# Layer 1 of a two-layer diffusion block: the first products of the feed-forward part by seven block products for eight, the gate row put into the second weights, and the attention values kept in float32

## The chip, the core and the metric

The kernel runs on one core of one Trainium2 chip. The metric is the device time of one execution in microseconds (us); lower is better. Names used below: PE is TensorE (matrix products), PEld its weight loads, DVE is VectorE, ACT is ScalarE, POOL is GpSimd, SP issues the DMAs. PSUM is the memory into which PE writes its sums, SBUF the memory from which every engine reads its operands.

## What is computed

One sample of 512 latent tokens (x) and 256 context tokens goes through two layers of width 1024, each with a mixer and a SwiGLU feed-forward part. All values are float32. Layer 0 works on all 768 tokens; behind layer 1's mixer only the 512 latent tokens are left.

```python
def _diff_attend(q, k, v, lam):              # layer 1: 8 heads, two score maps each
    s = einsum('bqhad,bkhad->bhaqk', q, k) * HEAD_DIM ** -0.5
    p = softmax(s)
    a = p[:, :, 0] - lam * p[:, :, 1]
    return einsum('bhqk,bkhe->bqhe', a, v)   # v: 128 wide

def _odd_mixer(...):
    q, k, v = split(h @ w_in)                # q and k: RMS norm by head, latent tokens rotated
    o = _rms(_diff_attend(q, k, v, lam), subln_w) * (1.0 - lam_init)
    return o @ w_out

def _swiglu(h, w_in, w_out):                 # w_in 1024 x 5632, w_out 2816 x 1024
    gate, up = split(h @ w_in, 2)
    return (silu(gate) * up) @ w_out

# per layer: x = x + gate1 * mixer(norm(x)); x = x + gate2 * swiglu(norm(x))
```

## The kernel before

**Precision.** A large product is made of three: each float32 operand is split into a rounded part ("hi", type fp32r) and the rest ("lo"), and PE adds hi x hi, hi x lo and lo x hi in PSUM. ACT makes hi (a cast), DVE or POOL makes lo (source minus hi). The same form splits weights (`unit`, L303 and L304), activations (`hT[0]` and `hT[1]`) and the hidden rows (`split`, L397 and L398). Products of plain float32 operands also exist: in layer 0 the attention's probabilities times values (L548); the trace has two instructions for each of those.

**Layer 1's mixer.** `in_proj1` runs over eight heads and six tiles of 128 tokens: 24 matmuls (L384 to L386), a copy out of PSUM (`qkv`), the values split into hi and lo (`vv`, L594 and L595), then `qk_norm_rope`: squares, sums by head, the inverse root on POOL (`rs_q`), the product with it on DVE (L363), then two products for q and two for k (L372, L374) and one sum. `attend1` makes two score maps per head and token tile, joins them (`e`), transposes six blocks of 128 x 128 on PE (`ppt`), splits them into `PTh` and `PTl` and multiplies: PTh by both parts of v (256 columns, L653) and PTl by the hi part of v (128 columns, L654). Two more operations add the halves.

**Layer 1's feed-forward part.** `norm_hT` first norms four tiles of tokens and writes them, transposed and split, into `hT`. `ffn` then loops over 11 pairs of 128-wide hidden blocks. For a pair it loads 512 KB pieces of gate and up weights and of the way out (`wgr`, `wur`, `wdr`) and splits them; for each block, PE makes gate and up for all 512 tokens (`pg`, `pu`: 8 k-steps x 3 matmuls of 512 columns, L738); ACT takes silu, DVE multiplies and splits into `hdh`, `hdl`. The way out is 8 half rows per pair (4 token tiles x 2 halves), 6 matmuls each into `dps` (L771 to L773); `residual` multiplies each by the gate row `g` (L391) and adds it to x (L392). In the first block gate and up are made for 256 tokens at a time, so that they can start before the last tiles are normed. The last two pairs share their way out. POOL does nothing in this loop.

**What sets the order.** A scheduler that plays the program through in its own model of time fixes the order on each engine when the kernel is built. Each engine then runs its list strictly in order, with semaphore waits. The number of buffers of each name (`bufs`) bounds how far one engine may run ahead of another.

Of the kernel before, what the change touches and what calls it, by code (L numbers as in the profile page):

```python
# [10 lines left out]
F32 = mybir.dt.float32  # L11
F32R = mybir.dt.float32r
# [6 lines left out]
P = 128  # L19
# [16 lines left out]
PBUF0 = 6  # L36
PBUF = 4
# [27 lines left out]
def backbone(es: ExitStack, tc: tile.TileContext, x, c, ctx, c_ctx, mod_w, mod_b, norm_mix_w, norm_ffn_w,  # L65
# [39 lines left out]
    def f32(ap):  # L105
        return ap.bitcast(F32)
# [38 lines left out]
    def rsqrt(ss, n, inv, tag):  # L145

        r = small.tile([P, n], F32, name="rs_" + tag, tag="rs_" + tag)
        nc.gpsimd.tensor_scalar(r, ss, inv, EPS, ALU.mult, ALU.add)
        nc.gpsimd.tensor_tensor(r, r, neghalf[:, :n], ALU.pow)
        return r  # L150
# [114 lines left out]

    def norm_steps(t, xt, l, f, pool, tags=(("nh", 2), ("nhc", 2)), room=None):
# [62 lines left out]

    def rotate(raw, nq, nk, t, w, tb, pool):  # L330
# [23 lines left out]
    def qk_norm_rope(ps, nq, nk, t, w, tb, pool):  # L354

        n = nq + nk
        sq = pool.tile([P, n * HD], F32, name="sq", tag="qz", bufs=2)
        nc.scalar.activation(sq, ps[:, :n * HD], AF.Square)
        ss = small.tile([P, n], F32, name="qss", tag="qss")
        nc.vector.tensor_reduce(ss, sq.rearrange("p (h d) -> p h d", d=HD), AX.X, ALU.add)  # L360
        r = rsqrt(ss, n, 1.0 / HD, "q")
        y = pool.tile([P, n, HD], F32, name="qy", tag="qy", bufs=2)
        nc.vector.tensor_tensor(y, ps[:, :n * HD].rearrange("p (h d) -> p h d", d=HD), bc(r, 2, HD), ALU.mult)  # L363
        parts = [p for p in ((0, 0, nq), (1, nq, nk)) if p[2]]
        if t >= NTX:
            for j, h0, m in parts:
                nc.vector.tensor_tensor(y[:, h0:h0 + m], y[:, h0:h0 + m], bc(w[:, j, :], 1, m), ALU.mult)
            return y
        z = pool.tile([P, n, HD], F32, name="qz", tag="qz", bufs=2)
        for j, h0, m in parts:  # L370
            sn = tb[:, j, t, 1, :].rearrange("p (a b) -> p a b", b=2)
            nc.vector.tensor_tensor(z[:, h0:h0 + m].rearrange("p h (a b) -> p h a b", b=2),  # L372
                                    swap_pairs(y[:, h0:h0 + m]), bc(sn, 1, m), ALU.mult)
            nc.vector.tensor_tensor(y[:, h0:h0 + m], y[:, h0:h0 + m], bc(tb[:, j, t, 0, :], 1, m), ALU.mult)  # L374
        nc.vector.tensor_add(y, y, z)
        return y

# [22 lines left out]

    def transposed_probs(Pt, heads, tiles, pool):

        res = []
        per = 4 // heads
        for g0 in range(0, len(tiles), per):
            grp = tiles[g0:g0 + per]
            m = len(grp)
            pt = tr_tile("ppt", [P, per, heads, P])
            for a, kc in enumerate(grp):
                for hh in range(heads):  # L410
                    nc.tensor.transpose(pt[:, a, hh, :], Pt[hh][:, kc * P:(kc + 1) * P], ident)
            hi, lo = split(pool, pt[:, :m], [P, m, heads, P], "PT", 2)
            for a in range(m):
                res.append((hi[:, a], lo[:, a]))
        return res
# [155 lines left out]
    def in_proj1(h, tabs, wp, st, wh, qp):  # L571
        w, tb = tabs
# [9 lines left out]
        vv = st.tile([P, NT, 2, P], F32R, name="vv", tag="vv")  # L582
# [3 lines left out]
        for t in CTX_FIRST:  # L586
            nq = 2 if t < NTX else 0
            n = 384 if nq else 256
# [4 lines left out]
            v = raw[:, n - P:n]  # L593
# [31 lines left out]
    def attend1(h, t, state, o_t, nlam, subln, mp):  # L625
# [22 lines left out]
        PT = transposed_probs(E[:1], 1, list(range(NT)), mp)  # L648
        av = acc_tile("av", 256, one=1)
        vt = [4, 5, 0, 1, 2, 3]  # L650
        for a, (hi, lo) in enumerate(PT):
            v = vv[:, vt[a]].rearrange("p a d -> p (a d)")
            nc.tensor.matmul(av, hi[:, 0], v, start=a == 0, stop=False)  # L653
            nc.tensor.matmul(av[:, 0:P], lo[:, 0], v[:, 0:P], start=False, stop=a == len(PT) - 1)  # L654
        o1 = mp.tile([P, P], F32, name="o1", tag="o1", bufs=2)
        nc.scalar.activation(o1, av[:, P:2 * P], AF.Copy, scale=rc[:, 0:1])
        oc = o_t[t][:, h * P:(h + 1) * P]
        nc.vector.scalar_tensor_tensor(oc, av[:, 0:P], rc[:, 0:1], o1, ALU.mult, ALU.add)
        ss = small.tile([P, 1], F32, name="oss", tag="oss")
# [50 lines left out]
    def ffn(l, xs, ntok, wp, fp, done, mods=()):  # L710
# [6 lines left out]
        for p in range(NF // 2):  # L717
# [59 lines left out]
            wo, hid = [], []  # L777

# [156 lines left out]
    tabs = rope_tables(wp.pool, od_qn[0], od_kn[0])  # L935
# [53 lines left out]
    room = ctx_room([P, 2, KT, P], F32, "nroom")  # L989
    for t in range(NTX):  # L990
        norm_hT(t, xs[t], 1, 1, None, room=[z[:, t % 2] for z in room])
# [65 lines left out]
```

## Time and profile before

| | us |
|---|---|
| time, median of 3 runs (1862.53 to 1865.8) | 1865.1 |
| time of the profiled execution | 1865.25 |
| its span, first to last instruction | 1863.5 |
| PE busy in the span | 1760.2 |
| DVE busy | 1162.2 |
| POOL busy | 789.8 |
| ACT busy | 716.5 |

1.75 us of the profiled execution lie outside its span. Busy times of one engine overlap with those of the others. The durations of single matmuls overlap too (the next starts while the last drains), so that the pace of PE is read from starts, or from a run of n matmuls in the chain of waits, and not from the mean duration. The stages in the trace, by their place in the span: layer 0's mixer up to about 450 us, its feed-forward part to 1012, layer 1's mixer and way out to 1476, the norm and the loop of layer 1's feed-forward part from there to the end.

### The profile page before, as it was taken

The page shows a single profiled execution, that of the slowest core. Times are in us where ns is not written, and L with a number is a line of the kernel's source. Part 1 is how long each engine was busy: PE and PEld are TensorE (multiplying, and loading weights), DVE is VectorE, ACT ScalarE, POOL GpSimd, SP SyncE. Part 2 cuts the span into 40 slices and gives each one's busy share as a digit, 9 for nine tenths or more (in the row PEclk, how much of TensorE's full clock was granted, in tenths as well). Part 3 has the DMA queues.
Part 4 walks back from the last instruction along what each step waited for, and adds up shares of the span by engine and source line. Part 5 has one row for each costly group of instructions (what it writes and reads, how often), then busy time and mean ns, then how long its engine had stood idle before and what let it go on. Part 6 is the DMA issues. An engine that isn't in the chain of part 4 may idle for free.

```text
span 1863.5 us, 25986 instructions
## 1 busy us (share of the span) xinstructions
PE 1760.2 (94%) x9910; PEld 1459.6 (78%) x9910; DVE 1162.2 (62%) x1927; ACT 716.5 (38%) x1470; POOL 789.8 (42%) x852
## 2 busy tenths in 40 slices
PE   6999999998999999899999889999998899999998
PEld 4877776666778888788888788999886688888887
DVE  4665455445268876667771767888876556566563
ACT  6556555434211112112211555676665332222220
POOL 2864545521099986735561655655543200000000
PEclk9999999999999999999999889999999899999999
DMA  9112222302533234424330211111103133223231
GB/s 314 42 41 77 83 93 91 100 23 81 180 114 101 93 100 146 138 91 136 103 124 14 96 38 57 35 38 48 49 19 107 46 113 108 85 91 113 69 113 46
DMA packets 152477, 165.64 MB, mean 89 GB/s; under 512 B 16480, under 2 KB 139936, under 8 KB 152352
## 3 DMA queue, kind: packets, MB, share of 16 engines
q1 hardware_dynamic: 152000, 163.77, 27.6%
q8 instruction: 78, 1.28, 0.3%
q14 instruction: 47, 0.39, 0.1%
q10 hardware_dynamic: 352, 0.21, 0.0%
HBM read 159.73 MB, written 4.22 MB: 88 GB/s over the span
## 4 chain that ended last, share of the span: by engine, by line
PE 74%; DVE 9%; ACT 5%; POOL 4%; DMA 3%; issue 3%; SPq 0%; POOLq 0%; ACTq 0%; DVEq 0%
PE pg L738 14%; PE pu L738 14%; PE dps L771 5%; PE dps L773 5%; PE dps L772 5%; PE inps L384 4%; PE inps L385 3%; PE inps L386 3%; PE av L548 3%; PE ppt L538 2%; PE sc L504 2%; PE ops L705 2%; PE ops L707 2%; PE ops L706 2%; PE av L653 1%
## 5 line engine op out<-in xcount | busy, mean ns | idle before, releaser
L738 PE MATMUL pg<-hT,wgh 128*128 128x512 f32 (+1 forms) x720 | 246.6, 391 | 3.1 <-ACT hT L288 3.1
L738 PE MATMUL pu<-hT,wuh 128*128 128x512 f32 (+1 forms) x720 | 243.2, 388 | 0.0
L391 DVE TENSOR_TENSOR rtmp<-dps,g 128x512 f32<-128x512 f32 x200 | 135.8, 687 | 163.7 <-PE dps L773 162.0
L392 DVE TENSOR_TENSOR x<-x,rtmp 128x512 f32<-128x512 f32 x188 | 198.8, 1065 | 3.8
L771 PE MATMUL dps<-wdh,hdh 128*128 128x512 f32 x440 | 177.1, 403 | 2.2 <-DVE rtmp L391 2.2
L772 PE MATMUL dps<-wdl,hdh 128*128 128x512 f32 x440 | 174.8, 397 | 0.0
L773 PE MATMUL dps<-wdh,hdl 128*128 128x512 f32 x440 | 171.9, 398 | 1.6 <-DVE hdl L398 1.6
L738 PEld LDWEIGHTS pg<-hT,wgh 128*128 128x128 f32 x720 | 135.4, 190 | 34.4 <-ACT hT L288 3.3
L738 PEld LDWEIGHTS pu<-hT,wuh 128*128 128x128 f32 x720 | 134.2, 188 | 29.6
L738 PE MATMUL pg<-hT,wgl 128*128 128x512 f32 (+1 forms) x360 | 141.4, 393 | 0.0
L738 PE MATMUL pu<-hT,wul 128*128 128x512 f32 (+1 forms) x360 | 139.7, 388 | 0.0
L384 PE MATMUL inps<-wih,hT 128*128 128x384 f32 x384 | 132.9, 346 | 0.4 <-ACT qkv L446 0.2
L397 ACT CAST hdh<-sg 128x768 fp32r<-128x768 f32 (+1 forms) x44 | 32.0, 728 | 256.5 <-DVE sg L753 256.5
L386 PE MATMUL inps<-wih,hT 128*128 128x384 f32 x384 | 130.3, 339 | 0.0
L385 PE MATMUL inps<-wil,hT 128*128 128x384 f32 x384 | 130.2, 339 | 0.0
L197 POOL TENSOR_TENSOR modw<-modw,cols 128x1024 f32<-128x1024 f32 x48 | 100.8, 2103 | 54.0 <-DMA modw<-in_mod_w_dram 53.7
L738 PE MATMUL pg<-hTc,wgh 128*128 128x256 f32 x352 | 99.5, 287 | 3.1 <-ACT hTc L288 2.4
L528 POOL TENSOR_SCALAR Pt<-Pt,rc 128x256 f32<-128x256 f32 (+3 forms) x96 | 69.2, 733 | 77.0 <-DVE rc L525 64.9
L771 PEld LDWEIGHTS dps<-wdh,hdh 128*128 128x128 f32 x440 | 83.2, 189 | 23.0 <-DVE rtmp L391 3.4
L773 PEld LDWEIGHTS dps<-wdh,hdl 128*128 128x128 f32 x440 | 83.0, 189 | 22.2 <-DVE hdl L398 2.3
L738 PE MATMUL pu<-hTc,wuh 128*128 128x256 f32 x352 | 98.1, 283 | 0.0
L772 PEld LDWEIGHTS dps<-wdl,hdh 128*128 128x128 f32 x440 | 83.3, 189 | 17.5
(230 smaller groups left out, 4486.3 us busy)
## 6 DMA issues: line engine op xcount, KB each, us to landing
modw<-in_mod_w_dram SPq DMA_DIRECT2D x96, 512.0 KB, 4.3
wgr<-in_ffn_w_in_dram SPq DMA_DIRECT2D x44, 512.0 KB, 3.4
wur<-in_ffn_w_in_dram SPq DMA_DIRECT2D x44, 512.0 KB, 3.5
wdr<-in_ffn_w_out_dram SPq DMA_DIRECT2D x44, 512.0 KB, 3.6
wir<-in_od_w_in_dram SPq DMA_DIRECT2D x96, 128.0 KB, 2.2
x<-in_x_dram SPq DMA_DIRECT2D x8, 512.0 KB, 3.5
wir<-in_ev_w_in_dram SPq DMA_DIRECT2D x16, 256.0 KB, 2.7
wor<-in_ev_w_out_dram SPq DMA_DIRECT2D x8, 512.0 KB, 4.3
```

What stands on the lines that cost most here:

```text
L197: nc.gpsimd.tensor_tensor(pr, w, bc(sk, 2, width), ALU.mult)
L384: nc.tensor.matmul(ps, hs[0][:, k, :], a, start=k == 0, stop=False)
L385: nc.tensor.matmul(ps, hs[0][:, k, :], b, start=False, stop=False)
L386: nc.tensor.matmul(ps, hs[1][:, k, :], a, start=False, stop=k == KT - 1)
L391: nc.vector.tensor_mul(tmp, ps, g[:, n * 512:(n + 1) * 512])
L392: eng.tensor_add(xt[:, n * 512:(n + 1) * 512], xt[:, n * 512:(n + 1) * 512], tmp)
L528: nc.gpsimd.tensor_scalar(p[:, :n], p[:, :n], rc[:, hh:hh + 1], 1.0, ALU.mult, ALU.mult)
L548: nc.tensor.matmul(av[64 * j:64 * j + 64, :], vv[:, vt[kc], :], PT[:, 2 * j:2 * j + 2].rearrange("p h q -> p (h q)"), start=kc == 0, stop= ...
L738: nc.tensor.matmul(ps[:, s0:s1], a, cols_T(b, s0, s1)[:, k, :], start=k == 0 and q == 0, stop=k == KT - 1 and q == 2)
L771: nc.tensor.matmul(ps, hh, a, start=j == 0, stop=False)
L772: nc.tensor.matmul(ps, hh, b, start=False, stop=False)
L773: nc.tensor.matmul(ps, hl, a, start=False, stop=j == nj - 1)
```

## The change

Layer 0 is left as it is. In layer 1:

**1. Seven products.** Gate (and, apart from it, up) of a pair is a product of a weight block of 1024 x 256 with the normed tokens, 1024 x 512. Both are cut in two along each side, and the four blocks of the result are made of seven products instead of eight (Strassen's scheme in Winograd's form). `seven_h` makes the seven token-side operands B once: four sums of blocks, and hi and lo of each. `seven_weights` makes the seven weight-side operands for each pair: four sums on POOL (`ss`, 128 x 512 elements each), and hi on ACT and lo on DVE of all seven (`sh`, `sl`, in a ring of 8). `seven_products` runs 12 matmuls of 256 columns for each product (L848), and DVE and ACT put the four blocks of the result together from PSUM (`u`, `c`). The scores' two PSUM tiles (`bank`) hold the seven products; gate and up use the same ones in turn.

**2. The gate row.** POOL multiplies the way out's weights by the gate row (L936) ahead of their split; `way_out` then needs one sum per half row (L922) where `residual` had a product and a sum.

**3. The norm.** `norm_raw` leaves the normed tokens in float32 (`hr`); their split moved into `seven_h`.

**4. Values in float32.** `vv` is one float32 copy (POOL), the transposed probabilities `PT` are copied once (ACT for four blocks, DVE for two) and multiplied in plain float32, 128 columns each (L679). One ACT operation scales the result.

**5. The norm and rotation of q and k.** `head_tables` stores the tables for q and k side by side, so that `rotate_all` needs two products and one sum for all four halves; POOL multiplies by the inverse root behind them.

```diff
+RING7 = 8
...
-        vv = st.tile([P, NT, 2, P], F32R, name="vv", tag="vv")
+        vv = st.tile([P, NT, P], F32, name="vv", tag="vv")
...
-            nc.scalar.copy(vv[:, t, 0, :], v)
-            nc.gpsimd.tensor_sub(vv[:, t, 1, :], v, f32(vv[:, t, 0, :]))
-            y = qk_norm_rope(raw, nq, 2, t, w, tb, wp)
+            nc.gpsimd.tensor_copy(vv[:, t, :], raw[:, n - P:n])
+            y, r = rotate_all(raw[:, :n - P], h0, m, t, wc, tb, wp)
+            nc.gpsimd.tensor_tensor(y, y, bc(r, 2, HD), ALU.mult)
...
-        PT = transposed_probs(E[:1], 1, list(range(NT)), mp)
-            nc.tensor.matmul(av, hi[:, 0], v, start=a == 0, stop=False)
-            nc.tensor.matmul(av[:, 0:P], lo[:, 0], v[:, 0:P], start=False, stop=a == len(PT) - 1)
...
+            if g0:
+                nc.vector.tensor_copy(PT[:, :m], pt[:, :m])
+            else:
+                nc.scalar.copy(PT, pt)
+            for a in range(m):
+                kc = g0 + a
+                nc.tensor.matmul(av, PT[:, a, :], vv[:, vt[kc], :], start=kc == 0, stop=kc == NT - 1)
...
+    ORDER7 = ("P1", "P2", "P5", "P6", "P7", "P3", "P4")
+    def seven_weights(raw, ring, room):
...
+            hi = ring.tile([P, 4, P], F32R, name="sh", tag="sh", bufs=RING7)
+            lo = ring.tile([P, 4, P], F32R, name="sl", tag="sl", bufs=RING7)
+            nc.scalar.copy(hi, src)
+            nc.vector.tensor_sub(lo, src, f32(hi))
...
+        s1 = made(a21, a22, ALU.add)          # made: nc.gpsimd.tensor_tensor
+        s2 = made(s1, a11, ALU.subtract)
+        s3 = made(a11, a21, ALU.subtract)
+        s4 = made(a12, s2, ALU.subtract)
...
+    def seven_products(ws, B, bank, n, room):
+        for name, (whi, wlo) in zip(ORDER7, ws):
+            for k in range(4):
+                for a, b, q in ((whi, bhi, 0), (whi, blo, 1), (wlo, bhi, 2)):
+                    nc.tensor.matmul(ps, a[:, k, :], b[:, k, :], start=k == 0 and q == 0, stop=k == 3 and q == 2)
+            if name == "P1":
+                nc.scalar.copy(u[:, 0, :], ps)
+            elif name == "P2":
+                nc.vector.tensor_add(c[:, 0, :], ps, u[:, 0, :])
+            elif name == "P6":
+                nc.vector.tensor_add(u[:, 1, :], ps, u[:, 0, :])
+            elif name == "P7":
+                nc.vector.tensor_add(u[:, 2:4, :], bank[0][:, 1, :, :n], bc(u[:, 1, :], 1, 2))
+                nc.vector.tensor_add(c[:, 3, :], ps, u[:, 2, :])
+        nc.vector.tensor_add(c[:, 1:3, :], bank[1][:, 0, :, :n], u[:, 2:4, :])
...
+    def seven_h(HR, room):
+        B["P1"] = parts(b11, place(0, 0, 0), place(1, 0, 0))
+        B["P2"] = parts(b21, place(0, 1, 0), place(1, 1, 0))
+        nc.vector.tensor_sub(b11, b12, b11)
+        B["P5"] = parts(b11, place(0, 0, 1), place(1, 0, 1))
+        nc.gpsimd.tensor_sub(b12, b22, b12)
+        B["P3"] = parts(b22, place(0, 1, 1), place(1, 1, 1))
+        nc.vector.tensor_sub(b22, b22, b11)
+        B["P6"] = parts(b22, *two(keep, "t2", tag="xo", bufs=6))
+        nc.vector.tensor_sub(b21, b21, b22)
+        B["P7"] = parts(b12, *two(room, "t3", tag="tt", bufs=4))
+        B["P4"] = parts(b21, *two(room, "t4", tag="tt", bufs=4))
...
+                nc.gpsimd.tensor_mul(raw, raw, g)          # way out's weights times gate row
...
+                    nc.vector.tensor_add(xh, xh, ps)       # way_out: one sum per half row
```

On DVE, in the loop of layer 1's feed-forward part, a stretch of a pair before: half rows of the way out (`rtmp`, `x_...`), the hidden rows (`hdl`) and pieces of the gate weights (`wgl`).

```order
L398 TENSOR_TENSOR hdl<-sg,hdh 128x512 [waits Activation_49]
L304 TENSOR_TENSOR wgl<-wgr,wgh 128x1024 [waits DMAHW0_49,PE_49,Activation_49]
L391 TENSOR_TENSOR rtmp<-dps,g_15389 128x512 [waits PE_49]
L392 TENSOR_TENSOR x_14893<-x_14893,rtmp 128x512 [waits DVE_49]
L391 TENSOR_TENSOR rtmp<-dps,g_15389 128x512 [waits PE_49]
L392 TENSOR_TENSOR x_14893<-x_14893,rtmp 128x512 [waits DVE_49]
L304 TENSOR_TENSOR wgl<-wgr,wgh 128x1024 [waits DMAHW1_49,PE_49,Activation_49]
```

The same engine at the same place with the change (`sl` is the lo part of a weight operand, `u` and `c` the sums out of PSUM, `x_...` the residual rows):

```order
L816 TENSOR_TENSOR sl<-ss,sh 128x512 [waits Activation_49]
L922 TENSOR_TENSOR x_14201<-x_14201,dps 128x512 [waits PE_49] x2
L816 TENSOR_TENSOR sl<-ss,sh 128x512 [waits PE_49,Activation_49] x2
L922 TENSOR_TENSOR x_14323<-x_14323,dps 128x512 [waits PE_49] x2
L856 TENSOR_TENSOR u<-bank,u 128x512 [waits DVE_49,PE_49]
L816 TENSOR_TENSOR sl<-wu,sh 128x512 [waits Activation_49]
L857 TENSOR_TENSOR c<-bank,u 128x256 [waits DVE_49]
L922 TENSOR_TENSOR x_14445<-x_14445,dps 128x512 [waits PE_49]
L858 TENSOR_TENSOR c<-bank,u 128x512 [waits PE_49]
```

The two-step residual became one step, and the lo parts and the sums out of PSUM now stand between the half rows, each behind a wait for ACT or PE.

On POOL, which in layer 1's loop had no rows before, one pair now reads (`ss` the sums of weight blocks, `wdr` the way out's weights times the gate row):

```order
L821 TENSOR_TENSOR ss<-wu 128x512 [waits DMAHW1_49,DVE_49,Pool_49]
L936 TENSOR_TENSOR wdr<-wdr,g_14734 128x1024 [waits DMAHW2_49]
L821 TENSOR_TENSOR ss<-ss,wu 128x512 [waits DVE_49,Pool_49]
L821 TENSOR_TENSOR ss<-wu 128x512 [waits DVE_49]
L936 TENSOR_TENSOR wdr<-wdr,g_14734 128x1024 [waits DMAHW3_49]
L821 TENSOR_TENSOR ss<-wu,ss 128x512 [waits DVE_49,Pool_49]
```

So POOL stands between the DMA and the splits on ACT and DVE for eight weight sums and two products a pair (the four sums of `wg` are like those of `wu`).

On PE in layer 1's mixer, before, the products of one head and token tile with the values:

```order
L654 MATMUL av<-vv,PTl 128x128 [waits DVE_49]
L653 MATMUL av<-vv,PTh 128x256
L654 MATMUL av<-vv,PTl 128x128
L653 MATMUL av<-vv,PTh 128x256
L654 MATMUL av<-vv,PTl 128x128
L653 MATMUL av<-vv,PTh 128x256
L654 MATMUL av<-vv,PTl 128x128
```

And with the change:

```order
L679 MATMUL av<-vv,PT 128x128 [waits Activation_49]
L679 MATMUL av<-vv,PT 128x128 x3
L671 MATMUL ppt<-cst,e 128x128 [waits PE_49]
L671 MATMUL ppt<-cst,e 128x128 x3
L679 MATMUL av<-vv,PT 128x128 [waits DVE_49]
L679 MATMUL av<-vv,PT 128x128
```

The first four blocks now wait for ACT's copy alone, the last two for DVE's; no lo part is waited for. Each row of L679 is a float32 product, which the trace will show as two instructions.

More of the change, by code (lines that the diff above doesn't have):

```diff
@@ L352, in rotate @@
         return y, r
[L354 to L376, printed above, removed]
     def project(ps, t, ws, c0, c1):
@@ L399, in split @@
         return hi, lo
[L401 to L415, printed above, removed]
     def weights0(b, wp, sub, new_tile=raw_tile):
@@ L586, in in_proj1 @@
         for t in CTX_FIRST:
[L587 to L588 removed]
+            h0 = 0 if t < NTX else 2
+            m = 4 - h0
+            n = 64 * m + P
             ps = acc_tile("inps", n, one=0) if h else p_sc.tile([P, 1024], F32, name="inps", tag="sc")[:, :n]
@@ new lines, in seven_h, with parts, place, two @@
+    def seven_h(HR, room):
+        def parts(src, hi, lo):
+            nc.scalar.copy(hi, src)
+            nc.vector.tensor_sub(lo, src, f32(hi))
+            return hi, lo
+        def place(j, ks, c):
+            return hT[j][0][:, 4 * ks:4 * ks + 4, 256 * c:256 * c + 256]
+        def two(pool, name, **kw):
+            return [pool.tile([P, 4, 256], F32R, name=name, **kw) for _ in range(2)]
+        b11, b21 = HR[0][:, 0:4], HR[0][:, 4:8]
+        b12, b22 = HR[1][:, 0:4], HR[1][:, 4:8]
+        B = {}
+        B["P1"] = parts(b11, place(0, 0, 0), place(1, 0, 0))
[9 more added lines that the diff above has]
+        B["P4"] = parts(b21, *two(room, "t4", tag="tt", bufs=4))
+        return B
@@ L988, in backbone @@
         oproj.sums(t)
-    room = ctx_room([P, 2, KT, P], F32, "nroom")
-    for t in range(NTX):
-        norm_hT(t, xs[t], 1, 1, None, room=[z[:, t % 2] for z in room])
     opa.close()
```

165 lines of the change are left out of this document (152 added, 13 removed).

## The prediction

> **What bounds the kernel now.** I read the busy times by stage first, since the change touches only the last two stages.
>
> ```profile
> 505.00:1012.00 507.00, 496.46 (x2659) 419.04 (x2658) 340.68 (x345) 89.35 (x104) 334.58 (x224) 0.99 0.34 109
> 1012.00:1085.00 73.00, 66.81 (x344) 57.59 (x343) 45.21 (x102) 34.26 (x58) 39.77 (x45) 0.93 0.20 64
> 1085.00:1400.00 315.00, 293.05 (x1964) 277.74 (x1962) 254.31 (x536) 205.62 (x562) 172.41 (x255) 0.96 0.14 42
> 1476.00:1512.00 36.00, 27.85 (x163) 24.82 (x163) 23.43 (x37) 18.20 (x20) 2.27 (x2) 0.86 0.46 147
> 1512.00:1843.00 331.00, 330.45 (x1418) 265.56 (x1417) 189.91 (x244) 80.53 (x96) 0.00 (x0) 1.00 0.27 86
> ```
>
> After the stretch and its length stand PE, PEld, DVE, ACT and POOL busy, PE's granted clock and the DMA share. From 1512 us on, in the loop of layer 1's feed-forward part, PE is busy for 330.45 of 331 us at full clock, DVE for 189.91, POOL not at all. That loop is bound by PE, and what it costs is the number of matmuls times their pace. The mixer (1012 to 1400) is less clear: PE sits idle for 6.2 + 21.95 = 28.1 us there, and DVE is at 81% in the longer stretch.
>
> The pace comes from the chain of waits, whose rows give the start and length of runs of matmuls:
>
> ```profile
> 1491.43 2.71 PE pu L738 x23
> 1494.49 2.71 PE pg L738 x23
> 1499.91 5.60 PE pg L738 x24
> 1505.51 5.59 PE pu L738 x24
> 1561.48 2.56 PE pg L738 x11
> 1628.64 2.56 PE pg L738 x11
> ```
>
> The first two rows are the first block, made for 256 tokens at a time: 2.71/23 = 0.118 us a matmul. The next two are of 512 columns: 5.60/24 = 0.233 us. The last two are the same place two pairs apart: 67.16 us, 33.58 us a pair. A pair before has 96 matmuls for gate and up and 48 for the way out, all of 512 columns: 144 x 0.233 = 33.6 us, which is the measured period.
>
> **The loop: PE.** A pair now has 14 products of 12 matmuls, 168 of 256 columns: 168 x 0.118 = 19.8 us for 96 x 0.233 = 22.4 us. The way out's 11.2 us stay. If PE remains the bound, a pair takes 31.0 us, 2.6 less; 11 pairs give 28 us. The price rests on the two 256-column rows, where every matmul loads a fresh weight tile, as in the seven products. The page "TensorE: Matmul & The Clock Gate" of the Trainium skill (section LDWEIGHTS) gives columns/1.2, an estimate of 107 ns for 128 columns, under the pace; those rows agree with it.
>
> **The loop: DVE and POOL.** These are the engines that take over what PE sheds.
>
> ```profile
> L391 DVE TENSOR_TENSOR rtmp<-dps,g 128x512 f32<-128x512 f32 x74 | 50.2, 690 | 74.5 <-PE dps L773 74.5
> L392 DVE TENSOR_TENSOR x<-x,rtmp 128x512 f32<-128x512 f32 x74 | 50.1, 688 | 1.3
> L304 DVE TENSOR_TENSOR wdl<-wdr,wdh 128x1024 fp32r<-128x1024 f32 x19 | 23.3, 1225 | 17.5 <-ACT wdh L303 17.5
> L304 DVE TENSOR_TENSOR wgl<-wgr,wgh 128x1024 fp32r<-128x1024 f32 x18 | 22.0, 1223 | 20.6 <-ACT wgh L303 20.6
> L398 DVE TENSOR_TENSOR hdl<-sg,hdh 128x512 fp32r<-128x512 f32 x21 | 14.5, 690 | 8.6 <-ACT hdh L397 8.2
> L375 DVE TENSOR_TENSOR qy<-qy,qz x32: 407/418/426, 1077.5 to 1387.3; 128x256 f32<-128x256 f32 x32
> L198 POOL TENSOR_TENSOR modp<-modp x16: 1263/1293/2280, 515.2 to 686.1; 128x512 f32<-128x512 f32 x16
> L197 POOL TENSOR_TENSOR modw<-modw,cols x48: 1889/1894/2873, 516.4 to 960.8; 128x1024 f32<-128x1024 f32 x48
> ```
>
> The first five are DVE's groups between 1512 and 1843 us, with POOL idle (count, busy us, mean ns); the others are single lines with minimum, median and maximum. A pair now gives DVE 30 operations of 512 elements (14 lo parts, 8 half rows, 4 sums out of PSUM, 2 products with up, 2 hidden lo parts), 2 of 1024 and 6 sums of 256. That is 30 x 0.69 + 2 x 1.225 + 6 x 0.418 = 25.7 us. Before it was 20 x 0.69 + 6 x 1.22 = 21.1 us. POOL gets 8 sums and 2 products: 8 x 1.263 + 2 x 1.889 = 13.9 us. Both fit under 31.0 us alone. But in layer 0's loop, where POOL is busy, the same DVE operations are longer (520 to 1000 us):
>
> ```profile
> L392 DVE TENSOR_TENSOR x<-x,rtmp 128x512 f32<-128x512 f32 x108 | 144.5, 1344 | 2.3
> L391 DVE TENSOR_TENSOR rtmp<-dps,g 128x512 f32<-128x512 f32 x108 | 73.3, 684 | 65.5 <-PE dps L773 63.8 <-DMA g<-gmem 1.7
> L304 DVE TENSOR_TENSOR wdl<-wdr,wdh 128x1024 fp32r<-128x1024 f32 x18 | 29.6, 1644 | 19.8 <-ACT wdh L303 19.8
> L304 DVE TENSOR_TENSOR wgl<-wgr,wgh 128x1024 fp32r<-128x1024 f32 x18 | 26.8, 1489 | 3.2 <-ACT wgh L303 3.2
> 520.00:1000.00 480.00, 469.46 (x2490) 396.66 (x2489) 339.40 (x342) 86.98 (x100) 327.88 (x220) 0.99 0.35 111
> ```
>
> The operation with both inputs in SBUF (x plus rtmp) takes 1344 for 688 ns, the one that reads PSUM 684, as before. With 18 `wul` counted like `wgl`, the excess is 108 x 0.656 + 18 x 0.419 + 36 x 0.266 = 88 us over 162 operations, 0.54 us each, at a POOL share of 327.88/480 = 68%. In the new loop 20 operations of a pair have both inputs in SBUF (18 of 512, 2 of 1024: 14.9 us), and POOL is at 13.9/32 = 43%: 20 x 0.54 x 43/68 = 6.8 us. DVE then needs 32.5 us, less what consecutive operations overlap, about 1 us (before, 21.1 us a pair by this count are 189.91 x 33.58/331 = 19.3 busy, part of it the few half rows missing in the stretch): 31.5 us, level with PE's 31.0. Two engines so close, each in order and waiting for the other, don't mesh perfectly; I take **32.0 us** a pair, an estimate: 11 x (33.58 - 32.0) = **-17.4 us**. Bounds: 31.0 (-28 us) below; above, all 20 paying the 0.656 of the row: 25.7 + 13.1 - 1 = 37.8 us a pair (+46 us).
>
> The page "SBUF — State Buffer" (section "SBUF: two separate sides") speaks against the change: DVE with two SBUF inputs and POOL hold one port pair by an exclusive lock for a whole instruction. The excess on `x<-x,rtmp` alone and not on `rtmp<-dps,g` agrees. What that would make of the time is the second rival.
>
> ACT's 80.53 us are 8.2 us a pair; 14 casts of 512 for 4 of 1024 and two copies less than double that. The DMA carries the same bytes at 27% busy. Both cost nothing. If ACT or a load were late, the ring of 8 operands covers about 8 x 12 x 0.118 = 11 us.
>
> **The start of the loop.**
>
> ```profile
> 1475.27 0.70 DVE L391 TENSOR_TENSOR ops<-ops,g 128x512 f32<-128x512 f32 x1
> 1486.62 1.22 DVE L289 TENSOR_TENSOR hT<-nroom,hT 128x1024 fp32r<-128x1024 f32 x1 [2.83 <-ACT hT L288]
> 1487.32 0.56 PE L738 MATMUL pg<-hT,wgh 128*128 128x256 f32 x1
> 1490.17 1.36 DVE L285 TENSOR_SCALAR nroom<-npt,aff,modc 128x128 f32<-128x128 f32 x4
> ```
>
> The last half row in front of the norm reaches DVE at 1475.27; PE starts on the loop at 1487.3 and covers the end of the last tile's norm (1491.5) with the first 256 tokens. The seven products allow less of that: five of the token operands need all four tiles. Behind the last norm DVE has three sums and five lo parts of 1024 (8 x 1.22 = 9.8 us), of which PE can cover two products (24 x 0.118 = 2.8 us). If the last tile is normed at 1487 (DVE no longer splits in between) to 1491.5, the last operand is there at 1497 to 1502, and the first seven products (9.9 us) end 1.4 us later: as if PE had started at 1488 to 1494. I take **+6 us**, with the DVE work for the first weights queued behind it; bounds -1 and +15.
>
> **The mixer.**
>
> ```profile
> 1240.43 0.22 PE L654 MATMUL av<-vv,PTl 128*128 128x128 f32 x1
> 1240.48 0.34 PE L653 MATMUL av<-vv,PTh 128*128 128x256 f32 x1
> 1240.66 0.23 PE L654 MATMUL av<-vv,PTl 128*128 128x128 f32 x1
> 1241.83 0.62 PE L411 MATMUL ppt<-cst,e 128*128 128x128 f32 x4
> 1242.21 0.36 PE L634 MATMUL sc<-kT,qt 128*128 128x256 f32 x1
> 280.45 1.08 PE L548 MATMUL av<-PT,vv 128*64 128x256 f32 x8
> 281.46 0.66 PE L538 MATMUL ppt<-cst,Pt 128*128 128x128 f32 x4
> L372 DVE TENSOR_TENSOR qz<-qy,rt 128x128 f32<-128x128 f32 x60 | 25.5, 465 | 0.6
> L374 DVE TENSOR_TENSOR qy<-qy,rt 128x128 f32<-128x128 f32 x60 | 18.8, 339 | 0.0
> L363 DVE TENSOR_TENSOR qy<-qkv,rs_q 128x256 f32<-128x256 f32 x30 | 21.5, 716 | 5.5 <-POOL rs_q L149 5.5
> PE av L654 <- DVE PTl L398: 7.6, 11, 2.9
> ```
>
> By starts, a block's two products take 0.23 us, 1.4 us for six. The new ones are float32: 12 instructions. Their price stands between a float32 transpose (0.38/4 = 0.095) and layer 0's float32 products (1.01/8 = 0.126): 1.1 to 1.5 us. For 32 head tiles -10 to +4 us; the first product behind a change of operand type seems to lose some 0.1 us (an estimate), so -8 to +10, and I take +3. In return DVE loses about half of L372 and L374 (two operations become one of 256; 22 us) and L363 (21.5 us), and the lo part becomes a copy of two blocks in six: over 45 of its 254 us in 1085 to 1400. PE's wait for `PTl` (7.6 us) goes. I let PE regain a third of the 28.1 us idle: -9. Net **-6 us**, bounds -25 and +12. POOL's new products with the inverse root (44 there, at most half of the 512 row's 1.26 us each: 28 us) fit beside its 172 of 315 us.
>
> **The end.** One DVE step of 0.69 us less behind the last matmul: **-0.7 us**.
>
> **The sum.** Against the profiled execution's own 1865.25 us (0.15 above the median of 1865.1): -17.4 + 6 - 6 - 0.7 = -18.1, **1847 us**.
>
> **Rivals.** *PE stays the bound outright*: a pair at 31.0, 11 us less than forecast, **1836**. For it: POOL's share would be lower than the 68% from which the excess was scaled. Against: 31.5 us of DVE work. *The port makes DVE the bound*: POOL and DVE work on the same weights at the same time, so the excess per operation doesn't shrink with POOL's share but stays at layer 0's 0.54 us. DVE then needs 25.7 - 1 + 20 x 0.54 = 35.5 us a pair, +1.9 x 11 = +21 instead of -17.4: **1886**, slower. It decides from 33.6 us a pair, where loop and forecast's other terms cancel: an excess of 0.45 us. For it: both rows of `x<-x,rtmp`; against: in layer 0 POOL hardly ever pauses. *The mixer loses*: products at the upper price and new waits for POOL's product with the inverse root, +12 for -6: **1865**. For it: PE's idle time there has many small causes, none over 7.6 us in the waits. *The change doesn't do what it says*: 256-column matmuls paced by a weight load's 190 ns (row below) would be 168 x 0.19 = 31.9 us for 19.8, +133 us or **1980**; the rows at 0.118 us, with a load each, all but exclude it.
>
> ```profile
> L738 PEld LDWEIGHTS pg<-hT,wgh 128*128 128x128 f32 x720 | 135.4, 190 | 34.4 <-ACT hT L288 3.3 <-issue 1.2
> ```
>
> **How the numbers follow.** Forecast 0.42 (its own range 1839 to 1857), PE the bound 0.18, the port 0.25, the mixer 0.14, the weight load 0.01. The range of 1831 to 1884 takes in the forecast, the mixer, most of the first rival and the nearer half of the port's; some 0.18 is left out. A difference under 0.2% (3.7 us) can't be told from none here. Faster: the forecast, the first rival and a little of the mixer, 0.61; same: half of the mixer, 0.08; slower: 0.31.
>
> **What would show it.** In the profile after: the period of a pair (33.58 us before) near 32; PE's idle time in the loop put down to `sl` (DVE) or to DVE's reads of `bank`; `sl` over 0.9 us in the mean for the port, near 0.69 without it. The forecast is wrong if 256-column matmuls leave 0.118 us, if DVE's busy share in the loop stays under 85% (then PE is the bound), or if the mixer moves by more than 15 us.

## The result and the profile after

| | before | after |
|---|---|---|
| median, on the same chip | 1863.8 us (4 runs) | 1921.1 us (4 runs) |
| profiled execution, and its span | 1865.25, 1863.5 | 1917.72, 1915.8 |

The ratio is 1.031, 95% interval 1.028 to 1.034: the change makes the kernel 57 us slower, outside the range of 1831 to 1884. In the profiled spans it is 52.3 us. Where they lie is read first by stage. These are the windows of the kernel after, with the columns of the prediction's first fence (PE, PEld, DVE, ACT, POOL busy, PE's clock, DMA share):

```profile
1085.00:1400.00 315.00, 293.06 (x2009) 277.70 (x2008) 223.43 (x390) 198.19 (x510) 196.06 (x307) 0.98 0.16 47
1463.00:1520.00 57.00, 32.80 (x202) 29.20 (x201) 52.08 (x73) 29.57 (x41) 29.82 (x21) 0.79 0.27 93
1641.95:1829.30 187.35, 164.74 (x1081) 153.44 (x1081) 151.49 (x191) 67.89 (x110) 85.04 (x51) 0.93 0.26 85
```

The last row is the steady part of the loop. PE, which was busy for 330.45 of 331 us there, is now at 88%, DVE at 81%, POOL at 45%, and PE's clock is 0.93. No engine is full. The period is read from ACT's silu, which comes once a pair; these two rows of its timeline are six pairs apart:

```profile
1624.55 1.15 ACT L942 ACTIVATE c<-c 128x512 f32<-128x512 f32 x2 [2.05 <-DVE c L858]
1849.62 1.15 ACT L942 ACTIVATE c<-c 128x512 f32<-128x512 f32 x2 [2.04 <-DVE c L858]
```

225.07/6 = 37.5 us a pair, 3.9 more than the 33.58 before: 11 x 3.9 = +43 us. The mixer ends earlier: the last matmul ahead of the norm, by its tile `ops` in the kernel before and after (minimum, median, maximum, then first and last start):

```profile
L707 PE MATMUL ops<-woh,hT x128: 388/396/793, 339.7 to 1474.8; 128*128 128x512 f32 x128
```

```profile
L731 PE MATMUL ops<-woh,hT x128: 389/396/774, 341.0 to 1462.6; 128*128 128x512 f32 x128
```

That is -12.2 us. The rest, 52.3 - 43 + 12.2 = +21.5 us, belongs to the start and end of the last stage.

**Where PE waits.** PE's waits from 1480 us on:

```profile
PE bank L848 <- DVE c L857: 45.1, 12, 6.7
PE bank L848 <- DVE hT L865: 4.4, 1, 4.4
PE bank L848 <- ACT hT L864: 3.5, 1, 3.5
PE bank L848 <- ACT u L850: 3.3, 1, 3.3
PE dps L918 <- ACT hdh L430: 3.2, 1, 3.2
```

One wait makes up 45 us: a product's first matmul waits for `c` (L857), DVE's read of P7, twelve times. It is no wait for an operand (`sl`). The timeline of one pair shows it on PE, then on DVE, then on POOL (start, length, idle time before and its releaser):

```profile
1749.44 0.28 PE L848 MATMUL bank<-t,sl 128*128 128x256 f32 x1
1754.24 0.80 PE L848 MATMUL bank<-hT,sh 128*128 128x256 f32 x2 [4.53 <-DVE c L857]
1754.84 0.41 PE L848 MATMUL bank<-hT,sl 128*128 128x256 f32 x1
1755.05 0.63 PE L848 MATMUL bank<-hT,sh 128*128 128x256 f32 x2
...
1743.23 1.83 DVE L939 TENSOR_TENSOR wdl<-wdr,wdh 128x1024 fp32r<-128x1024 f32 x1
1744.98 0.41 DVE L852 TENSOR_TENSOR c<-bank,u 128x256 f32<-128x256 f32 x1
1745.31 1.21 DVE L939 TENSOR_TENSOR wdl<-wdr,wdh 128x1024 fp32r<-128x1024 f32 x1
1746.44 2.98 DVE L816 TENSOR_TENSOR sl<-ss,sh 128x512 fp32r<-128x512 f32 x3
1749.35 2.83 DVE L816 TENSOR_TENSOR sl<-wg,sh 128x512 fp32r<-128x512 f32 x1
1752.11 0.68 DVE L856 TENSOR_TENSOR u<-bank,u 128x512 f32<-128x512 f32 x1
1752.71 1.15 DVE L816 TENSOR_TENSOR sl<-wu,sh 128x512 fp32r<-128x512 f32 x1
1753.78 0.41 DVE L857 TENSOR_TENSOR c<-bank,u 128x256 f32<-128x256 f32 x1
...
1747.26 1.62 POOL L821 TENSOR_TENSOR ss<-wu 128x512 f32<-128x512 f32 x1 [3.28 <-issue]
1748.84 2.79 POOL L936 TENSOR_TENSOR wdr<-wdr,g 128x1024 f32<-128x1024 f32 x1
1751.59 1.71 POOL L821 TENSOR_TENSOR ss<-ss,wu 128x512 f32<-128x512 f32 x1
```

The reads of PSUM (L856, L857) stand in DVE's list behind two `wdl` and four `sl`. Most of them meet an operation of POOL: the `sl` at 1749.35 takes 2.83 us for 0.69 and ends at 1752.18, 0.55 us behind POOL's product with the gate row (1748.84 + 2.79 = 1751.63). DVE makes no pause from 1743.23 to the end of L857 at 1754.19, so that it isn't late by waiting for POOL's results there. At the pace of e4's trace (0.60 us from start to start for 512 elements, 2.27 for two `wdl`) the same operations would take 6.6 us for these 11.0, an estimate. PE finished P7 at 1749.7 and stands until 1754.24. Behind the wait, three matmuls take 0.64 us where they took 0.36 (0.118 each), for 3 to 4 us. A pair is so 31.0 us of PE's work, 4.5 of waiting and 2 of slow clock.

Why does PE wait for a read of P7 at all? In the built order the products of the up set stand on PE as P1, P6, P2, P3, P4, P5, P7, and right behind P7 comes the next gate set's P1. P1 writes other columns than P7, but both lie in the same tile, `bank[0]`, and the wait is for the tile's last reader. The up set's P1 waits for such a read as well, but half rows of the way out stand in front of it and keep PE busy; so PE stands once a pair and not twice.

**How large the contention is.** DVE's groups over five pairs (1642 to 1829 us; count, busy us, mean ns):

```profile
L816 DVE TENSOR_TENSOR sl<-ss,sh 128x512 fp32r<-128x512 f32 x40 | 32.8, 838 | 9.3 <-ACT sh L815 8.7
L816 DVE TENSOR_TENSOR sl<-wg,sh 128x512 fp32r<-128x512 f32 x15 | 21.0, 1402 | 5.1 <-ACT sh L815 5.1
L947 DVE TENSOR_TENSOR c<-c 128x512 f32<-128x512 f32 x10 | 17.5, 1792 | 0.2
L939 DVE TENSOR_TENSOR wdl<-wdr,wdh 128x1024 fp32r<-128x1024 f32 x10 | 15.2, 1518 | 0.0
L816 DVE TENSOR_TENSOR sl<-wu,sh 128x512 fp32r<-128x512 f32 x15 | 12.5, 835 | 0.0
L856 DVE TENSOR_TENSOR u<-bank,u 128x512 f32<-128x512 f32 x10 | 6.8, 684 | 2.5 <-PE bank L848 2.5
```

Against 0.69 and 1.225 us, the first five lose 40 x 0.15 + 15 x 0.71 + 10 x 1.10 + 10 x 0.29 + 15 x 0.145 = 32.7 us, 6.5 us a pair; the read of PSUM (684 ns) loses nothing. The forecast had 6.8.

### The profile page after: what moved, and what is told of

It reads as the page before. It is cut to its first block, busy times and chain, and to the rows that moved or that the text cites. A ratio compares the mean times of both kernels' runs of the same rounds, so it can differ in the third digit from the quotient of the medians.

```text
span 1915.8 us, 27843 instructions
## 1 busy us (share of the span) xinstructions
PE 1756.1 (92%) x10654; PEld 1498.4 (78%) x10654; DVE 1248.7 (65%) x1909; ACT 754.5 (39%) x1525; POOL 1002.1 (52%) x1011
## 5 line engine op out<-in xcount | busy, mean ns | idle before, releaser
L848 PE MATMUL bank<-hT,sh 128*128 128x256 f32 x704 | 144.4, 302 | 58.9 <-DVE c L857 45.1
L848 PEld LDWEIGHTS bank<-hT,sh 128*128 128x128 f32 x704 | 121.0, 206 | 67.7 <-DVE c L857 48.0
L762 PE MATMUL pg<-hT,wgh 128*128 128x512 f32 x352 | 131.3, 394 | 0.0
L762 PE MATMUL pu<-hT,wuh 128*128 128x512 f32 x352 | 130.2, 391 | 0.0
L848 PE MATMUL bank<-t,sh 128*128 128x256 f32 x528 | 108.0, 300 | 1.3 <-DVE t L865 1.3
L848 PE MATMUL bank<-hT,sl 128*128 128x256 f32 x352 | 105.5, 300 | 0.0
L796 PE MATMUL dps<-wdl,hdh 128*128 128x512 f32 x264 | 104.9, 397 | 0.0
L848 PEld LDWEIGHTS bank<-t,sh 128*128 128x128 f32 x528 | 91.6, 210 | 2.9 <-DVE t L865 1.6
L816 DVE TENSOR_TENSOR sl<-ss,sh 128x512 fp32r<-128x512 f32 x88 | 79.6, 922 | 17.4 <-ACT sh L815 16.2
L322 POOL TENSOR_TENSOR wil<-wir,wih 128x768 fp32r<-128x768 f32 x42 | 79.3, 1894 | 14.2 <-ACT wih L321 13.0
## 6 DMA issues: line engine op xcount, KB each, us to landing
wir<-in_od_w_in_dram SPq DMA_DIRECT2D x96, 128.0 KB, 2.2
```

The lines of the kernel that those rows point to most:

```text
L762: nc.tensor.matmul(ps[:, s0:s1], a, cols_T(b, s0, s1)[:, k, :], start=k == 0 and q == 0, stop=k == KT - 1 and q == 2)
L796: nc.tensor.matmul(ps, hh, b, start=False, stop=False)
L816: nc.vector.tensor_sub(lo, src, f32(hi))
L848: nc.tensor.matmul(ps, a[:, k, :], b[:, k, :], start=k == 0 and q == 0, stop=k == 3 and q == 2)
```

## The experiments

Theories: **the port** (POOL's operations hold up DVE's) and **the shared tile and the list** (PE waits for reads that stand late in DVE's list, whatever makes the list late). All times are medians; "before" was 1862.7 to 1864.5 us beside them. In the table, "pair" is the time from the fourth silu of the loop to the tenth, over 6 (in e1, from PE's runs of `pg`); PE and DVE are busy us in 1620 to 1780 (160 us).

| run | time, us | ratio to before, 95% | pair | PE | DVE |
|---|---|---|---|---|---|
| after | 1921.1 | 1.028 to 1.034 | 37.5 | 141.9 | 128.0 |
| e1 mixer alone | 1855.2 | 0.993 to 0.996 | 33.6 | | |
| e2 no POOL work | 1866.7 | 1.001 to 1.002 | 33.0 | 153.1 | 116.3 |
| e3 no gate product | 1907.7 | 1.022 to 1.026 | 37.0 | 142.8 | 120.7 |
| e4 all on DVE | 1921.1 | 1.028 to 1.033 | 37.7 | 142.6 | 130.6 |
| e12 tiles split | 1890.3 | 1.013 to 1.017 | 34.8 | 148.0 | 141.6 |
| e5 more PSUM room | 1882.9 | 1.009 to 1.013 | 35.0 | 149.6 | 139.9 |
| e6 room, no POOL work | 1839.8 | 0.985 to 0.989 | 31.6 | 160.0 | 121.1 |
| e7 room, x divided | 1862.0 | 0.998 to 1.001 | 31.4 | 158.5 | 137.5 |
| e8 room, all on DVE | 1852.3 | 0.992 to 0.995 | 31.1 | 160.0 | 151.8 |
| e9 room, gate on POOL | 1856.8 | 0.994 to 0.997 | 31.7 | 158.1 | 156.5 |
| e10 as e8, norm on ACT | 1851.2 | 0.991 to 0.994 | 31.0 | 160.0 | 152.6 |
| e11 as e10, x divided | 1861.2 | 0.997 to 0.999 | 30.8 | 160.0 | 143.2 |

The silu's place within a pair floats; in e6, with PE busy throughout, the six intervals lie between 29.7 and 32.5 us, so that PE's column is the surer one there.

**e1: the mixer alone.** The changed kernel, with the norm and feed-forward part of before.

```diff
-    HR = ctx_room([P, KT, 256], F32, "hr")
...
-    ffn7(1, xs, HR, bank, wp.pool, fp.pool,
+    room = ctx_room([P, 2, KT, P], F32, "nroom")
+    for t in range(NTX):
+        norm_hT(t, xs[t], 1, 1, None, room=[z[:, t % 2] for z in room])
...
+    ffn(1, xs, NTX, wp.pool, fp.pool,
```

> The kernel before with parts 4 and 5 of the change alone (the mixer); norm and feed-forward part as before. In the trace after, the last matmul of the way out in front of the norm starts 12.2 us earlier than before (1462.6 for 1474.8 us). Theory 'the mixer gained what it shows and all of the loss is in the feed-forward part': 1863.8 - 12 = 1852 us, 1848 to 1856. Rival 'the earlier end is only shifted work, given back behind it': 1861 to 1866 us.

1855.2 us, inside the first theory's range and 9.3 us less than before beside it (6.7 to 13.2 by the interval). The mixer's gain is kept; the feed-forward change costs 1921.1 - 1855.2 = 66 us.

**e2 and e3: POOL's work left out.** Both keep the order of the operations on PE, ACT and DVE in the last nine of the eleven pairs; in the first two the scheduler built another one.

```diff
-                nc.gpsimd.tensor_mul(raw, raw, g)          # e2 and e3
...
-            s = room.tile([P, 4, P], F32, name="ss", tag="ss", bufs=3)
-            nc.gpsimd.tensor_tensor(s, a, b, op)
-            return s
+            return a                                        # e2 alone
```

> The changed kernel without POOL's work in the loop: the four sums of weight blocks are left out (each is replaced by its first block, so the products are of other numbers) and the product of the way out's weights with the gate row is left out. DVE, ACT and PE have the same operations in the same order in the loop as the changed kernel. Theory 'the port' (DVE's operations on two SBUF inputs lose time to POOL's, and the reads of PSUM queue behind them): the wait of 4.5 us before each gate or up product set goes, with the slow matmuls behind it; a pair falls from 37.4 to 31.0 to 31.8 us, sl to 0.69 us, the time to 1848 to 1865 us. Rival 'the list' (the sums out of PSUM stand behind five lo parts in DVE's list and are late whatever POOL does): the wait stays over 2 us, a pair at 34 us or more, 1885 us or more.

> The changed kernel without POOL's product of the way out's weights with the gate row (left out, so the gate doesn't act); the four sums stay on POOL. The same order on DVE. Theory 'the port', with the two 2.8 us products in the burst ahead of the late PSUM reads as its main part: the wait of 4.5 us falls to under 2 us, a pair to 33 to 35 us, 1870 to 1892 us. Variant 'the sums matter as much': a pair at 35 to 36.5 us, 1892 to 1910 us. Rival 'the list': 1912 to 1921 us.

e2 takes 54 us off, yet a pair stays at 33.0 us, between what the two theories gave. Its timeline on PE, and its waits from 1480 us on (`c` is L855 there):

```profile
1683.60 0.28 PE L846 MATMUL bank<-t,sl 128*128 128x256 f32 x1
1685.59 0.51 PE L846 MATMUL bank<-hT,sh 128*128 128x256 f32 x2 [1.72 <-DVE c L855]
1685.93 0.28 PE L846 MATMUL bank<-hT,sl 128*128 128x256 f32 x1
1686.05 0.40 PE L846 MATMUL bank<-hT,sh 128*128 128x256 f32 x2
```

```profile
PE bank L846 <- DVE c L855: 20.4, 11, 4.4
```

With POOL idle and DVE at 73%, PE still stands 1.7 us at the same place: P7 ends, DVE makes `u`, one `sl` and then `c`. Behind this shorter wait the matmuls keep their pace. So POOL's work is worth 4.5 of the 6.5 us that a pair takes over 31.0, and 2.0 are there without it. e3's time lies where the variant "the sums matter as much" had it, its pair (37.0) a little above: the gate product is 13 us of the 54, although it is a third of POOL's busy time. In the steady pairs it is 0.5 us of the 4.5, so that there nearly all of POOL's price comes from the sums. PE still waits at the same place, nine times of the eleven for 3.44 to 3.46 us (total, times and longest):

```profile
PE bank L848 <- DVE c L857: 34.1, 11, 3.5
```

**e4: POOL's work on DVE.**

```diff
-            nc.gpsimd.tensor_tensor(s, a, b, op)
+            nc.vector.tensor_tensor(s, a, b, op)
...
-                nc.gpsimd.tensor_mul(raw, raw, g)
+                nc.vector.tensor_mul(raw, raw, g)
```

> The changed kernel with POOL's sums and gate products moved to DVE; the same results. DVE then has 25.7 + 8 x 0.69 + 2 x 1.22 = 33.7 us a pair, about 32.7 with overlap, and no contention. Theory 'the port': DVE is the bound at 32.7 to 34 us a pair and POOL's help was worth nothing, 1866 to 1885 us, so that 5.5 us of work handed to POOL cost more than it saved. Rival 'DVE's amount of work and its order': with 8 us more in its list the PSUM reads are later still, a pair over 37.5 us, over 1920 us.

No contention is left, and the time is that of the changed kernel. The port theory as stated falls: it gave 1866 to 1885 us. DVE's timeline and PE's wait at its end:

```profile
1757.58 0.69 DVE L816 TENSOR_TENSOR sl<-ss,sh 128x512 fp32r<-128x512 f32 x1
1758.18 0.69 DVE L816 TENSOR_TENSOR sl<-wg,sh 128x512 fp32r<-128x512 f32 x1
1758.78 0.69 DVE L856 TENSOR_TENSOR u<-bank,u 128x512 f32<-128x512 f32 x1
1759.38 0.68 DVE L821 TENSOR_TENSOR ss<-ss,wu 128x512 f32<-128x512 f32 x1
1759.98 0.69 DVE L816 TENSOR_TENSOR sl<-wu,sh 128x512 fp32r<-128x512 f32 x1
1760.58 0.69 DVE L821 TENSOR_TENSOR ss<-wu 128x512 f32<-128x512 f32 x1
1761.18 0.42 DVE L857 TENSOR_TENSOR c<-bank,u 128x256 f32<-128x256 f32 x1
...
1761.66 0.51 PE L848 MATMUL bank<-hT,sh 128*128 128x256 f32 x2 [4.12 <-DVE c L857]
```

Every operation takes its undisturbed time; the sums that POOL made now stand in the list ahead of L857 (the scheduler built DVE's list anew). Whether POOL slows what is queued there or DVE has more queued there, PE waits the same 4 us.

**e12 and e5: the tiles.** e12 changes in the source only which tile a pair of products lies in. In e5 P1 and P6 share a tile, P2 has one, and P5, P7, P3 and P4 lie in one that takes turns with a second from set to set; L856 and L857 then stand behind P4. In both, two of the tiles are those of the transposes, and the gate row is made ahead of them.

```diff
-            ("P1", 0, 0), ("P2", 0, 1), ...        # bank[a // 2][:, a % 2, b, :n]
+            ("P1", 0, 0), ("P2", 0, 1), ...        # e12: bank[a][:, b, :n], four tiles
...
+        big, one, two = bank[0], bank[2], bank[3]  # e5
+        bank[0], bank[1] = bank[1], bank[0]        # the other tile for the next set
+        into = {"P1": one[:, 0, :n], "P6": one[:, 1, :n], "P2": two[:, 0, :n],
+                "P5": big[:, 0, 0, :n], "P7": big[:, 0, 1, :n], "P3": big[:, 1, 0, :n], "P4": big[:, 1, 1, :n]}
```

> The changed kernel with its seven products in the same pairs of PSUM slots (P1 with P2, P5 with P7, P3 with P4, P6), but each pair in a tile of its own instead of two pairs to a tile; no second set of room, the same sums in the same places, POOL's work as in the changed kernel. P1 of the next set then waits for the readers of P1 and P2 alone, and P5 for those of P5 and P7. Theory 'shared tiles': most of what the larger room gave (38 us) comes from the split alone: a pair at 34.5 to 36 us, 1880 to 1897 us. Rival 'too little room': the second set of P5, P7, P3 and P4 was what helped, and the split alone leaves a pair at 36.5 us or more, 1905 us or more.

> The changed kernel with other PSUM room for the seven products, and no other change of its work: P5, P7, P3 and P4 of a set in one tile, the next set's in a second one, P1 with P6 and P2 in two further tiles (those of the transposes, free in the loop). A product of the next set then waits for no sum of this one. Without POOL's work the pair was still 33.0 us, 2.0 over PE's own 31.0, with a wait of 1.7 us for c (L857) at each P1 that follows a P7. Theory 'shared PSUM tiles': the wait of 4.5 us and the slow matmuls behind it go almost wholly, whatever POOL does; DVE's busy time of 30.3 us a pair and PE's 31.0 give 31.5 to 33.5 us, 1858 to 1880 us. Theory 'the port': DVE, slowed by POOL, is the bound wherever the wait stands; a pair at 35 us or more, 1895 us or more.

e12 lies inside the first theory's range: the split takes 31 us off, e5's room 7 more, by intervals that just don't touch. PE's waits in e12 from 1463 us on, of which the first and the fifth row:

```profile
PE dps L919 <- DVE hdl L431: 10.7, 9, 2.7
PE bank L848 <- DVE c L857: 4.7, 3, 2.2
```

The waits for L857 fall from 45.1 us to 4.7: the long wait went with the shared tile. But the 31 us aren't shown to be the tile's alone. With the tiles apart the scheduler also built another order on PE and DVE: at 1741.92 in e12 the gate set's L856 follows right on the hidden rows (`hdl`), where the changed kernel has four `sl` and four half rows between them. No run changed the tiles in a fixed order, or moved the reads forward in DVE's list with the tiles shared, so the two shares aren't shown apart. The same holds for e5 to e11, whose orders differ from the changed kernel's too.

e5's time is 3 us above its range and a pair, at 35.0, is where the port theory had it. DVE's groups in e5 (1600 to 1800 us) show why:

```profile
L816 DVE TENSOR_TENSOR sl<-ss,sh 128x512 fp32r<-128x512 f32 x46 | 45.2, 996 | 5.0 <-ACT sh L815 5.0
L431 DVE TENSOR_TENSOR hdl<-c,hdh 128x512 fp32r<-128x512 f32 x11 | 17.4, 1611 | 0.0
L947 DVE TENSOR_TENSOR c<-c 128x512 f32<-128x512 f32 x10 | 15.2, 1556 | 0.0
```

Against 0.69 us these lose 46 x 0.306 + 11 x 0.921 + 10 x 0.866 = 32.9 us, and the other lo parts 4.8: 6.6 us a pair, as much as in the changed kernel. The loss has only moved, in part to the hidden rows, which lost nothing before (677 ns). POOL still has a pause of some 8 us in a pair; it is busy for 80.6 of 160 us, before for 68.0. PE's waits are now spread over `x`, `c`, `hdh` and `hdl`.

**e6 to e8: the room with less, or none, of POOL's work.** e6 is e5 without POOL's work (as e2), e8 is e5 with it on DVE (as e4). e7 leaves the sums on POOL and takes the gate row out of the loop:

```diff
+        nc.vector.reciprocal(ig, g)
+        for t in range(NTX):
+            nc.gpsimd.tensor_mul(xs[t], xs[t], ig)
...
-                nc.gpsimd.tensor_mul(raw, raw, g)
...
                     if last:
+                        nc.vector.tensor_mul(xh, xh, g[:, n * 512:(n + 1) * 512])
```

> The PSUM room of the run before together with POOL's work left out (the four sums and the gate product, as in the run without POOL's work). Theory 'shared PSUM tiles': the 1.7 us wait goes, PE is the bound: a pair at 31.0 to 31.3 us, 1841 to 1850 us. Rival 'the lists' (PE and DVE in order, whatever the tiles): a pair stays at 32.5 us or more, 1862 us or more.

> The PSUM room with all of POOL's work of the loop on DVE (same results). DVE's busy time was 31.0 us a pair with this work (61.98 of 74.5 us for two pairs) and PE's own pace is 31.0. Theory 'shared PSUM tiles': 31.3 to 33 us a pair, 1852 to 1872 us, since DVE's amount of work alone doesn't make 37 us. Rival 'DVE's amount of work': it stays over 35 us a pair, 1895 us or more.

> The PSUM room of the first run of this call, and the gate row taken out of the loop: x is divided by the gate row ahead of the loop (a reciprocal on DVE, four products on POOL) and multiplied by it behind the last sum; POOL keeps the four sums a product set, some 11 us a pair instead of 17. If the port still costs time once PE no longer waits for PSUM, this is 5 to 20 us faster than the run with PSUM room alone: 1848 to 1862 us, a pair at 31.0 to 32 us. If it costs nothing any more: the same within 3 us, the end 0.7 us longer. It would be the fastest version if it ends under the mixer alone (1855 us).

e6 ends a little below the first theory's range, e8 inside it, e7 at the upper end of its own. The windows of e6, then of e8:

```profile
1620.00:1780.00 160.00, 160.00 (x1108) 149.15 (x1108) 121.05 (x196) 68.14 (x115) 0.00 (x0) 1.00 0.33 105
```

```profile
1620.00:1780.00 160.00, 160.00 (x1115) 149.36 (x1114) 151.79 (x246) 67.96 (x114) 0.00 (x0) 1.00 0.31 99
```

In both PE has no gap, at full clock; in e8 DVE is at 95% and it doesn't matter, because nothing on PE waits closely for it. The same operations as in e4, in another order, take 69 us less. e8 is faster than e5 by 31 us although DVE has 8 us more of its own work a pair: POOL's help was a loss. e7 ends at the time of before; its pair is 31.4 us, but its reciprocal and POOL's four products fall into the start (in 1490 to 1520 DVE is busy for 29.0 us, PE for 19.4).

**e9 to e11: towards a faster version.** e9 is e8 with the gate product on POOL. e10 is e8 with half of the norm's scale and shift on ACT; e11 adds e7's division.

```diff
+                if g == 0:
+                    nc.scalar.activation(hc[:, kk, :], pt[:, k, :], AF.Identity, scale=aff[l][:, f, kk, i:i + 1],
+                                         bias=modc[l][:, 3 * f, kk, i:i + 1])
```

> PSUM room, the four sums a set on DVE, the gate product left on POOL (the only work of POOL in the loop). Theory 'the port': POOL's two products of 1.89 us a pair keep DVE waiting about as long as DVE would need to make them itself (2 x 1.22 us), so handing them over gains nothing: 1850 to 1860 us against 1852.3 with all on DVE. Rival 'POOL's help is real once the sums are gone': DVE at 28.5 us a pair, 1843 to 1849 us.

> PSUM room and all sums and gate products on DVE, and in the norm ahead of the loop half of the scale-and-shift operations (four of eight blocks of each tile) moved from DVE to ACT, which was busy for half of that stretch. Theory 'DVE bounds the start' (24.4 of 25 us busy in 1465 to 1490, PE at 9.9): 16 operations of 0.39 us, 5.2 us by their pace of 1.36 us for four, leave DVE and the loop starts 3 to 5 us earlier: 1847 to 1849.5 us. Rival 'ACT or a load bounds it too': no change, 1851 to 1854 us.

> As the run before, with the gate row out of the loop: x divided by the gate row ahead of the loop (a reciprocal on DVE, four products of 1024 on POOL) and multiplied by it behind the last sum; sums on DVE. DVE falls to about 28.5 us a pair against PE's 31.0, but DVE gets a reciprocal at the start, where it is the bound, POOL's four products lie there too, and the end has one DVE step more. If the pair was held over 31.0 by DVE: 1842 to 1847 us; if the start takes it back: 1848 to 1856 us.

e9: with the product on POOL the time is 4 us more than with it on DVE, by intervals that touch, so that nothing is gained; DVE is busier with it (156.5 for 151.8 us in the same 160), since it waits for POOL's 2.74 us operations. e10 is 1.1 us under e8, within what the runs can tell, so that the theory "DVE bounds the start" isn't borne out: DVE's busy time in 1465 to 1490 fell from 24.4 to 20.0 us, and PE's longest waits in e10 from 1465 us on name ACT.

```profile
PE npt L278 <- ACT nh L274: 8.5, 2, 4.6
PE bank L854 <- ACT u L856: 5.4, 1, 5.4
PE npt L278 <- ACT hr L282: 4.1, 2, 2.7
```

e11 has the shortest pair (30.8 us) and gives it back at the start: at 1861.2 us it lies above both ranges that were given for it. e10 is the fastest version that computes everything, 0.8% under before; e8 and e10 differ from the mixer alone by 3 and 4 us, with intervals that touch.

## Why the prediction was wrong

**The step that failed** is in "The loop: DVE and POOL": "Two engines so close, each in order and waiting for the other, don't mesh perfectly; I take 32.0 us a pair". The sums behind it held. PE's work is 31.0 us a pair (e6, e8); DVE's was put at 24.7 without contention, and e2 has 24.0 in a pair of 33.0; the contention was put at 6.8 us, and 6.5 were measured. What the sum of busy times can't hold is the coupling. Once a pair the gate set's P1 waited for a read of P7; the two reads of that tile stood behind two `wdl` and four `sl` in DVE's list, so DVE's lateness there became PE's idle time with DVE at 81%. The "imperfect mesh" was taken as 0.5 to 1 us; it was 6.5, 4.5 of them idle and 2 of slow clock. The two PSUM tiles were named as the kernel's, and never priced. Of the 70.6 us between the 1847 forecast and the 1917.7 profiled, this term has 60 (+43 for -17.4), the start of the loop some 16, and the mixer gives 6 back.

**The rivals.** "The port makes DVE the bound" (35.5 us, 1886) came nearest in time and sign. It was right that POOL slows DVE (e2: 4.5 us a pair, by the wait and the clock), and wrong in how that reaches PE: DVE was never full, and PE's idle time comes from one late read. With POOL's work on DVE, and so without contention, the time was the same (e4). Once the tiles are apart it has the number of e5, 35.0 us a pair where e8, with the work on DVE, has 31.1; but DVE is at 87% there, so that it isn't the bound in e5 either. "PE stays the bound" is what e6 and e8 show. The sign to read it by, "DVE's busy share under 85%: then PE is the bound", was false: DVE was at 81% and PE at 88%.

**Start of the loop.** Forecast +6 with bounds -1 and +15, and -0.7 at the end; measured +21.5 for both, outside the bounds. In 1463 to 1520 DVE is busy for 52.1 of 57 us and PE for 32.8, at a clock of 0.79. From the last matmul ahead of the norm to the end, less 11 pairs of PE's 31.0, e6 has 1839.8 - 1468.7 - 341 = 30 us where before has 1863.5 - 1474.8 - 11 x 33.58 = 19: so +11 is the price without POOL and without shared tiles, already twice the forecast. Made in the same way, each with its own pair, after has 41, e2 36 and e5 33: POOL's work and the shared tiles each have a part of the other 10. e8, with POOL's work on DVE, has 44, so that its loop at 31.1 us gains less than it could. What bounds the start stays open: e10 took 4.4 us of DVE's work away there, and its time is 1.1 us lower, which is within the scatter of the runs.

**The mixer.** Forecast -6; -12.2 in the trace and -9.3 alone (in the other runs of the same mixer the last matmul starts between 1461.5 and 1468.7 us, 6 to 13 us before 1474.8). Right in sign, within its bounds, too small by half. That DVE would shed over 45 of 254 us in 1085 to 1400 was too much (254.31 to 223.43: 31).

**The matmuls.** 256 columns kept 0.118 us each wherever the clock was full, as forecast.

## What to carry to other kernels

For every product, ask which reads its PSUM tile must be free of, and what stands ahead of those reads in the reader's list: two results in one tile make PE wait for both, and a split of the tile, with the order that the scheduler then built, was worth 31 us here with no operation changed. Sums of busy time give a loop's period only where the engines aren't chained so closely; e4 and e8 do the same work 69 us apart. An operation with two SBUF inputs that was handed from DVE to POOL wasn't taken off DVE: it came back as waiting. All on DVE was as fast with the shared tiles (1921.1 us both) and 31 us faster with the room.

## What the runs showed of the hardware

PE's clock falls within a steady loop: behind waits of 4.5 us the matmuls ran at 0.21 us for 0.118 for 3 to 4 us (granted clock 0.93 over the stretch), and still so behind the waits of 3.44 to 3.46 us of e3 (0.93); behind the 1.7 us waits of e2 the clock was 1.00. The Trainium skill's page "TensorE: Matmul & The Clock Gate" (Part 1) says that the clock halves after an idle window of about 3.4 us and recovers after as much of work; these runs agree.

POOL and DVE slow each other on operations with two SBUF inputs: the product of 1024 took 2.8 us on POOL for 1.89, `sl` up to 2.83 for 0.69, while DVE's reads of PSUM stayed at 0.68. The page "SBUF — State Buffer" of the Trainium skill (section "SBUF: two separate sides") calls it a lock held for the whole instruction. The `sl` that ended 0.55 us, less than its own 0.69, behind POOL's product agrees.
